# Weight splits of a float32 two-block network: six buffers instead of four for each split half, and a scheduling priority of 150 places for weight loads and splits

## The chip, the cores and the metric

One core of a Trainium2 chip runs the whole program. The metric is the device time of one execution in microseconds (us), and the kernel before is given by three runs and one profiled execution.

## The reference, cut to what matters

A sequence of 256 tokens of width 1024 goes through two layers of a first block (a pooling branch, sparse attention that keeps the 64 best keys of each query, attention to a memory, three gated merges), then through one layer of a second block (a gated delta rule run in both directions, a short convolution branch, a gated merge) and a gated MLP. Everything is float32. Nearly all of the arithmetic is a product of activations with a weight matrix:

```python
proj = h @ w_in[l]                                   # first block, 1024 x 6728 per layer
merged = (g[:, :, 0] * (y_pool @ w_branch[l, 0]) + g[:, :, 1] * (y_attn @ w_branch[l, 1])
          + g[:, :, 2] * (y_mem @ w_branch[l, 2]))
x = x + merged @ w_out[l]
...
o_dn = gated_deltanet_bidir(q, k, v, z, b_raw, a_raw, conv_w, A_log, dt_bias, norm_w)   # second block
h_res = h_res + (silu(gu[..., :D_FF]) * gu[..., D_FF:]) @ w_down[l]                     # MLP
```

## The kernel before, in words

**A product.** Every float32 product is computed as three products of a reduced-precision type: an operand is split into a high half H (its rounded copy) and a low half L (operand minus H), and the kernel sums H·H, H·L and L·H in PSUM (`mm3`, L116 to L124; `units`, L138 to L153). The activations are split once. The weights are read from HBM once and split on the way: `load` (L92 to L95) issues a DMA from SP into one of five `raw` buffers, and `weights` (L97 to L114) lets ScalarE write H (L107) and VectorE write L (L110), into one of four `wH` and one of four `wL` buffers. A part is up to four blocks of 128 rows by 256 columns, 128x1024 elements in a buffer. A unit of work is a weight block of 1024 rows by 256 columns: two parts, 48 matmuls on TensorE, two result tiles. In the second block and the MLP every third L is written by POOL (`pool_l`, L108 and L109).

**The order of the program.** Block 1 (`_block1`, L220) goes twice through projections, attention, branches and output. It begins with DMAs of `norm_g` (L258) and of x in four pieces (L261), with the first two half parts of weights between them (`K.ahead`, L263); then x is split (`xsplit`, L284), and two units are computed side by side (L333) while POOL sums the squares of x (L188 to L194). Block 2 (`_block2`, L575) begins with q, k and v and their convolutions (`qkv`, L659, VectorE at L685), and then interleaves further units (`z_unit`, `gate`, the `w_sc` units) with a generator, `delta` (L835): decays, an inverse of triangular blocks of 32 in many small VectorE steps (`inverse_blocks`, L820 to L832), a way through DRAM and back (L946 writes, `load_inverse` L988 to L1005 reads, all from SP), and then matmuls and VectorE steps per half of the heads. The generator is advanced by `K.pump` after each unit, and drained before the output product. `_mlp` (L1264) is products almost alone.

**What sets the order on an engine.** The program is traced in that order, and each instruction takes a place from it. The framework then goes through a modelled timeline and gives each engine, whenever it is free there, the ready instruction with the lowest place; an instruction that needs a buffer is ready once a buffer of its tag is free. What comes out is a fixed queue for each engine, which the chip executes in that order: an instruction that has to wait holds up all that stand behind it on its engine, SP's DMA queue included. The kernel asks for this with `schedule_with_timeline_sim=True` in `kernel` (L1417). `issue_after` (L75 to L81) adds that certain instructions are not put ahead of the last weight load or matmul traced so far.

Of the kernel before, what the change touches and what calls it, by code (L numbers as in the profile page):

```python
# [8 lines left out]
F32R = mybir.dt.float32r  # L9
# [20 lines left out]
RATE = 2.0  # L30
POOL_L = 3
NL0 = 1


def _constants():
# [16 lines left out]
class _K:  # L52
# [43 lines left out]

    def weights(self, blk, kt, n):  # L97

        nc = self.nc
        parts = {}  # L100
        k0 = 0
        while k0 < kt:
            raw = self.ahead.pop(0) if self.ahead else self.load(blk, k0, min(4, kt - k0), n)
            m = raw.shape[1]
            H = self.wp.tile([128, 4, n], F32R, tag="wH", name="wH", bufs=4)[:, :m, :]
            L = self.wp.tile([128, 4, n], F32R, tag="wL", name="wL", bufs=4)[:, :m, :]
            nc.scalar.activation(H, raw, AF.Copy)  # L107
            self.n_l += 1  # L108
            e = nc.gpsimd if self.pool_l and self.n_l % self.pool_l == 0 else nc.vector  # L109
            e.tensor_tensor(L, raw, H.bitcast(F32), op=OP.subtract)  # L110
            for i in range(m):
                parts[k0 + i] = H, L, i
            k0 += m
        return [lambda k, a=a: parts[k][a][:, parts[k][2], :] for a in range(2)]  # L114
# [59 lines left out]
    def hl(self, pool, src, shape, tag, bufs=1):  # L174
        nc = self.nc
        H = pool.tile(shape, F32R, tag=tag + "H", name=tag + "H", bufs=bufs)
        L = pool.tile(shape, F32R, tag=tag + "L", name=tag + "L", bufs=bufs)
        nc.scalar.activation(H, src, AF.Copy)
        nc.vector.tensor_tensor(L, src, H.bitcast(F32), op=OP.subtract)
        return H, L  # L180

    def scaled_hl(self, H, L, x, g):

        nc = self.nc
        nc.scalar.activation(H, x, AF.Copy, scale=g)
        nc.vector.scalar_tensor_tensor(L, x, g, H.bitcast(F32), op0=OP.mult, op1=OP.subtract)
# [388 lines left out]
def _block2(K, x):  # L575
# [19 lines left out]

    K.pool_l, K.n_l = POOL_L, NL0

# [833 lines left out]
```

## Time and profile before

| | |
|---|---|
| median of three runs | 1180.29 us (1178.58 to 1182.12) |
| the profiled execution's own time | 1179.4 us |
| its span, first to last instruction | 1177.4 us |
| mean granted TensorE clock | 0.979 |
| busy: TensorE, VectorE, ScalarE, POOL | 1114.1, 869.0, 586.7, 383.5 us |
| bytes read from HBM | 189.39 MB, 165 GB/s over the span |

The profiled execution lies 0.9 us under the median. The rows further down come from it. A busy TensorE means that matmuls are in flight; a clock of 1.00 is the higher of its two levels (2.4 GHz), and a mean below that is time at the lower one (1.2 GHz). In rows of a timeline the first two columns are the start and the duration in us, and square brackets give the idle time of the engine before the row and the instruction that ended it. In rows of waits, "A <- B: t, n, m" says that A waited for B for t us in total, n times, at most m.

### The profile page before, as it was taken

The page shows a single profiled execution, that of the slowest core. Times are in us where ns is not written, and L with a number is a line of the kernel's source. Part 1 is how long each engine was busy: PE and PEld are TensorE (multiplying, and loading weights), DVE is VectorE, ACT ScalarE, POOL GpSimd, SP SyncE. Part 2 cuts the span into 40 slices and gives each one's busy share as a digit, 9 for nine tenths or more (in the row PEclk, how much of TensorE's full clock was granted, in tenths as well). Part 3 has the DMA queues.
Part 4 walks back from the last instruction along what each step waited for, and adds up shares of the span by engine and source line. Part 5 has one row for each costly group of instructions (what it writes and reads, how often), then busy time and mean ns, then how long its engine had stood idle before and what let it go on. Part 6 is the DMA issues. An engine that isn't in the chain of part 4 may idle for free.

```text
span 1177.4 us, 23260 instructions
## 1 busy us (share of the span) xinstructions
PE 1114.1 (95%) x9536; PEld 1086.1 (92%) x9536; DVE 869.0 (74%) x1220; ACT 586.7 (50%) x883; POOL 383.5 (33%) x304
## 2 busy tenths in 40 slices
PE   6999999999999999999999878698899999999996
PEld 6999999999999999999998878697799999999996
DVE  8668897678665897977899899996547497555543
ACT  6344546446344454455675947242235645444442
POOL 8102310003100040100854668933011157534353
PEclk9999999999999999999999979898899999999999
DMA  7765453565655544455544525454432355556561
GB/s 262 268 211 170 156 173 123 180 192 182 196 192 182 179 133 136 147 177 180 186 169 144 181 82 144 134 175 105 148 126 94 134 187 180 200 172 199 180 193 40
DMA packets 68514, 194.63 MB, mean 165 GB/s; under 512 B 19504, under 2 KB 21816, under 8 KB 67896
## 3 DMA queue, kind: packets, MB, share of 16 engines
q1 hardware_dynamic: 66056, 188.72, 49.9%
q10 hardware_dynamic: 2352, 4.43, 1.1%
q8 instruction: 74, 1.21, 0.4%
q14 instruction: 32, 0.26, 0.1%
HBM read 189.39 MB, written 5.30 MB: 165 GB/s over the span
## 4 chain that ended last, share of the span: by engine, by line
PE 70%; DVE 17%; DMA 4%; issue 3%; ACT 2%; POOL 2%; SPq 1%; DVEq 0%; ACTq 0%; POOLq 0%
PE mm L123 49%; PE mml L151 8%; PE mmd L1302 5%; DVE wL L110 4%; DVE ac L685 2%; DVE Tb L830 1%; PE hp L372 1%; ACT wH L107 1%; DMA sT<-Lb 1%; DMA rows<-scr 1%; DVE tm L828 1%; DVE vf L685 1%; DVE kq L713 1%; PE mo L495 1%; PE vn L1088 1%
## 5 line engine op out<-in xcount | busy, mean ns | idle before, releaser
L110 DVE TENSOR_TENSOR wL<-raw,wH 128x1024 fp32r<-128x1024 f32 (+2 forms) x292 | 395.9, 1362 | 156.4 <-ACT wH L107 139.4
L107 ACT ACTIVATE wH<-raw 128x1024 fp32r<-128x1024 f32 (+3 forms) x347 | 347.0, 1034 | 302.4 <-PE mm L123 150.2
L123 PE MATMUL mm<-xH,wL 128*128 128x256 f32 (+3 forms) x1720 | 247.7, 284 | 11.2 <-DVE wL L110 11.2
L123 PE MATMUL mm<-xH,wH 128*128 128x256 f32 (+3 forms) x1720 | 249.0, 286 | 5.6 <-ACT ac L680 1.8
L123 PE MATMUL mm<-xL,wH 128*128 128x256 f32 (+3 forms) x1720 | 248.6, 285 | 0.0
L123 PEld LDWEIGHTS mm<-xH,wL 128*128 128x128 f32 (+1 forms) x1720 | 221.9, 190 | 13.5 <-DVE wL L110 12.3
L123 PEld LDWEIGHTS mm<-xH,wH 128*128 128x128 f32 (+1 forms) x1720 | 222.7, 190 | 9.5 <-ACT ac L680 2.0
L123 PEld LDWEIGHTS mm<-xL,wH 128*128 128x128 f32 (+1 forms) x1720 | 223.2, 191 | 2.8 <-issue 2.2
L110 POOL TENSOR_TENSOR wL<-raw,wH 128x1024 fp32r<-128x1024 f32 (+2 forms) x55 | 133.9, 2434 | 217.5 <-ACT wH L107 149.3
L397 POOL TENSOR_TENSOR bp<-bias,sc 128x1024 f32<-128x1024 f32 (+1 forms) x4 | 14.7, 3667 | 246.3 <-DVE sc L395 219.9
L123 PE MATMUL mm<-yH,wH 128*128 128x256 f32 x256 | 42.5, 286 | 4.9 <-ACT yH L1207 4.9
L123 PE MATMUL mm<-yL,wH 128*128 128x256 f32 x256 | 43.0, 286 | 4.3 <-DVE yL L1208 4.3
L123 PE MATMUL mm<-yH,wL 128*128 128x256 f32 x256 | 42.1, 285 | 0.0
L191 POOL TENSOR_TENSOR acc<-x 128x256 f32<-128x256 f32 x2 | 1.4, 722 | 123.6 <-DVE x L562 120.4
L123 PEld LDWEIGHTS mm<-yH,wH 128*128 128x128 f32 x256 | 35.6, 193 | 5.2 <-ACT yH L1207 5.1
L123 PEld LDWEIGHTS mm<-yL,wH 128*128 128x128 f32 x256 | 35.7, 193 | 5.1 <-DVE yL L1208 4.8
L123 PEld LDWEIGHTS mm<-yH,wL 128*128 128x128 f32 x256 | 35.5, 193 | 0.3 <-issue 0.3
L193 POOL TENSOR_TENSOR sq<-x 128x256 f32<-128x256 f32 x33 | 33.6, 1027 | 6.2 <-DVE x L562 5.5
L685 DVE SCALAR_TENSOR_TENSOR ac<-rc,cw,ac 128x271 f32<-128x271 f32 (+3 forms) x48 | 34.4, 753 | 0.0
L191 POOL TENSOR_TENSOR a<-x 128x256 f32<-128x256 f32 x3 | 2.8, 941 | 80.4 <-DVE x L562 74.8
L1302 PE MATMUL mmd<-aH,wH 128*128 128x256 f32 x176 | 28.6, 281 | 0.0
L1302 PE MATMUL mmd<-aH,wL 128*128 128x256 f32 x176 | 28.6, 281 | 0.0
(433 smaller groups left out, 1829.3 us busy)
## 6 DMA issues: line engine op xcount, KB each, us to landing
raw<-in_w_b SPq DMA_DIRECT2D x64, 512.0 KB, 4.1
raw<-in_w_a SPq DMA_DIRECT2D x55, 512.0 KB, 4.0
raw<-in_w_gu SPq DMA_DIRECT2D x44, 512.0 KB, 4.5
raw<-in_w_branch SPq DMA_DIRECT2D x24, 512.0 KB, 4.3
raw<-in_w_out SPq DMA_DIRECT2D x24, 512.0 KB, 3.8
raw<-in_w_qkv SPq DMA_DIRECT2D x24, 512.0 KB, 3.8
raw<-in_w_sc SPq DMA_DIRECT2D x24, 512.0 KB, 3.8
raw<-in_w_down SPq DMA_DIRECT2D x20, 512.0 KB, 4.4
```

The lines of the kernel that those rows point to most:

```text
L107: nc.scalar.activation(H, raw, AF.Copy)
L110: e.tensor_tensor(L, raw, H.bitcast(F32), op=OP.subtract)
L123: self.last_mm = nc.tensor.matmul(ps, lt(a, kt), rt(b, kt), start=i == 0, stop=i == n - 1).ins
L151: self.last_mm = self.nc.tensor.matmul(ps[:, :N], w[a](k)[:, h * 128:h * 128 + 128], xs[b][:, k, :], start=k == 0 and (a, b) == (0, 0), st ...
L193: nc.gpsimd.tensor_tensor(tmp, x, x, op=OP.mult)
L372: nc.tensor.matmul(pp[p][:, j, :n], a[r, 2 * i + j, :], b(r, 2 * i + j), start=True, stop=True)
L397: nc.gpsimd.tensor_tensor(bp[:, :, :n], bias[:, :, off:], pen[:, None, :n].to_broadcast([128, 8, n]), op=OP.add)
L495: nc.tensor.matmul(ps[:, h, :], mv[:, mb, h * 128:h * 128 + 128], PT[:, mb, h, :], start=mb == 0, stop=mb == 1)
L685: V.scalar_tensor_tensor(ac[:, t0:t1], r[:, t0 + j - 2:t1 + j - 2], w[:, j:j + 1], ac[:, t0:t1], op0=OP.mult, op1=OP.add)
L713: (V if (i * 8 + h) % 3 else G).tensor_tensor(t, t, sl(h, i), op=OP.mult)
L828: eng.tensor_tensor(t, Lb[:, j + 1:, j:j + 1].to_broadcast([P, m, w]), Tb[:, j:j + 1, 0:w].to_broadcast([P, m, w]), op=OP.mult)
L1302: nc.tensor.matmul(pss[h][:, :S], w[a](k)[:, h * 128:h * 128 + 128], (aH, aL)[b][:, k0 + k, :], start=k0 + k == 0 and (a, b) == (0, 0), st ...
```

## The change

Three edits. The body of `weights` becomes `split_weights`, and `weights` calls it with the scheduler's place of everything traced inside lowered by 150, so that a part's load (where it isn't one of the two `ahead` loads, which are issued elsewhere), its H and its L count as traced 150 instructions earlier than they were. The tags `wH` and `wL` get six buffers each instead of four; `raw` keeps five. And the region of each SBUF partition that is set aside for descriptors of DMAs issued by POOL is set to 512 bytes, which makes room for the four added buffers of 4 KB per partition each.

```diff
+AHEAD = 150
...
     def weights(self, blk, kt, n):
 
+        with self.tc.high_priority(AHEAD):
+            return self.split_weights(blk, kt, n)
+
+    def split_weights(self, blk, kt, n):
         nc = self.nc
...
-            H = self.wp.tile([128, 4, n], F32R, tag="wH", name="wH", bufs=4)[:, :m, :]
-            L = self.wp.tile([128, 4, n], F32R, tag="wL", name="wL", bufs=4)[:, :m, :]
+            H = self.wp.tile([128, 4, n], F32R, tag="wH", name="wH", bufs=6)[:, :m, :]
+            L = self.wp.tile([128, 4, n], F32R, tag="wL", name="wL", bufs=6)[:, :m, :]
...
-    nc = bacc.Bacc("TRN2", target_bir_lowering=False, num_devices=1)
+    nc = bacc.Bacc("TRN2", target_bir_lowering=False, num_devices=1, dynamic_dma_scratch_size=512)
```

## Rows read from the trace of the kernel before

**Rows 1.** The page, part 1: TensorE's busy time, share of the span and instructions.

```profile
PE 1114.1 (95%) x9536; PEld 1086.1 (92%) x9536; DVE 869.0 (74%) x1220; ACT 586.7 (50%) x883; POOL 383.5 (33%) x304
```

**Rows 2.** The table of windows, by stages: window and its length; busy us (and instructions) of TensorE, its weight loads, VectorE, ScalarE, POOL; granted clock; share of the DMA engines busy; GB/s.

```profile
0.00:60.00 60.00, 49.70 (x387) 47.26 (x387) 44.00 (x50) 30.47 (x45) 28.80 (x38) 1.00 0.78 267
60.00:480.00 420.00, 419.60 (x3566) 409.94 (x3567) 316.91 (x480) 204.07 (x311) 53.59 (x52) 1.00 0.54 171
480.00:512.00 32.00, 30.46 (x272) 29.46 (x271) 27.72 (x33) 16.50 (x33) 4.25 (x1) 1.00 0.46 147
...
585.00:805.00 220.00, 188.00 (x1409) 180.91 (x1407) 210.70 (x315) 129.58 (x223) 137.43 (x109) 0.94 0.47 148
805.00:831.00 26.00, 19.00 (x124) 17.28 (x125) 11.60 (x20) 7.19 (x11) 4.52 (x4) 0.80 0.58 156
831.00:990.00 159.00, 156.26 (x1677) 151.68 (x1677) 105.49 (x152) 72.75 (x96) 50.91 (x29) 0.98 0.41 134
```

**Rows 3.** Waits of TensorE in the stretch 585 to 831 us, the five longest in total.

```profile
PE mm L123 <- DVE wL L110: 8.6, 3, 5.6
PE ms L984 <- ACT mkv L980: 5.5, 1, 5.5
PE mm L123 <- ACT yH L1207: 4.9, 1, 4.9
PE mvn L979 <- DVE mkv L976: 4.7, 1, 4.7
PE mm L123 <- DVE yL L1208: 4.3, 1, 4.3
```

**Rows 4.** Waits over the whole span: what ScalarE's H split waited for most.

```profile
ACT wH L107 <- PE mm L123: 150.2, 68, 5.2
```

**Rows 5.** The chain of waits over the whole span (start, us, what): a stretch of TensorE in the MLP without a wait, in which 960 matmuls are 20 units.

```profile
991.52 113.06 PE mm L123 x960
```

**Rows 6.** Timeline of VectorE, 685 to 742 us: a convolution step that was held up, and the L split behind it.

```profile
694.61 7.43 DVE L685 SCALAR_TENSOR_TENSOR vf<-rc,cw,vf 128x270 f32<-128x270 f32 x1
701.96 1.29 DVE L110 TENSOR_TENSOR wL<-raw,wH 128x1024 fp32r<-128x1024 f32 x1
```

**Rows 7.** Timeline of POOL around the same moment: the first and the last but one of the six operations that it ran without a gap from 694.76 to 702.17 us.

```profile
694.76 1.89 POOL L897 TENSOR_TENSOR E<-Gb,Gt 128x1024 f32<-128x1024 f32 x1
...
699.41 2.33 POOL L110 TENSOR_TENSOR wL<-raw,wH 128x1024 fp32r<-128x1024 f32 x1
```

**Rows 8.** Timeline of TensorE: the product that waited for that L split.

```profile
703.30 1.23 PE L123 MATMUL mm<-xH,wL 128*128 128x258 f32 x4 [5.57 <-DVE wL L110]
```

**Rows 9.** SP's DMA issues around 805 us (start, us): the inverse on its way to DRAM and back (L946, L998 to L1003), and the next weights.

```profile
804.26 1.18 SPq L946 DMA_DIRECT2D sT<-Tb  x2
...
819.27 0.48 SPq L1000 DMA_DIRECT2D TBX<-sT  x1
...
823.22 0.98 SPq L94 DMA_DIRECT2D raw<-in_w_gate  x2
```

**Rows 10.** The chain of waits, 800 to 835 us (start, us, what).

```profile
805.49 11.27 DMA sT<-Lb
...
823.22 4.75 DMA raw<-in_w_gate
...
829.04 0.58 ACT mkv L980
```

**Rows 11.** Waits of ScalarE, 800 to 832 us.

```profile
ACT wH L107 <- DMA raw<-in_w_gate: 8.0, 1, 8.0
```

**Rows 12.** Waits of TensorE, 50 to 580 us.

```profile
PE mm L123 <- ACT wH L107: 0.8, 1, 0.8
PE mm L123 <- DVE wL L110: 0.7, 1, 0.7
```

**Rows 13.** SP's DMA issues at the start (start, us): the first piece of x, and the three whole parts of the two first units.

```profile
1.19 0.41 SPq L261 DMA_DIRECT2D x<-in_xT  x1
...
4.01 1.81 SPq L94 DMA_DIRECT2D raw<-in_w_a  x3
```

**Rows 14.** ScalarE at the start: the split of the first piece of x, and those of the first and the last of the three whole parts of weights, each begun when its data landed (the second began at 11.88 us).

```profile
4.48 0.91 ACT L185 ACTIVATE xH<-x,ng 128x256 fp32r<-128x256 f32 x2 [2.25 <-DMA x<-in_xT]
...
10.41 1.06 ACT L107 ACTIVATE wH<-raw 128x1024 fp32r<-128x1024 f32 x1 [0.33 <-DMA raw<-in_w_a]
...
13.24 1.39 ACT L107 ACTIVATE wH<-raw 128x1024 fp32r<-128x1024 f32 x2 [0.30 <-DMA raw<-in_w_a]
```

**Rows 15.** TensorE at the start: the first product, and the sum over the squares of x, which stands behind the last of the 96 products of the two first units.

```profile
6.30 0.79 PE L151 MATMUL mml<-xH,wH 128*128 128x256 f32 x2 [6.30 <-ACT wH L107]
...
21.09 0.59 PE L201 MATMUL stat<-acc,ones 128*128 128x256 f32 x2
```

**Rows 16.** Waits of TensorE, 0 to 60 us.

```profile
PE mm L123 <- DVE wL L110: 1.9, 2, 1.3
```

**Rows 17.** The L split (L110) on VectorE: count, ns min/median/max, first and last start.

```profile
L110 DVE TENSOR_TENSOR wL<-raw,wH x292: 351/1222/4916, 6.3 to 1154.7; 128x1024 fp32r<-128x1024 f32 x142, 128x288 fp32r<-128x288 f32 x2, 128x512 fp32r<-128x512 f32 x1, 128x192 fp32r<-128x192 f32 x1
```

**Rows 18.** The DMA queues (packets, MB, share of 16 engines): the two that carry what the program issues, from SP and from ScalarE; the list of issues by line names no other engine.

```profile
q1 hardware_dynamic: 66056, 188.72, 49.9%
q10 hardware_dynamic: 2352, 4.43, 1.1%
```

## The prediction

> **What bounds the kernel now.** I began with the page [rows 1]: TensorE is busy 1114.1 of 1177.4 us, so 63.3 us idle are all that better feeding can win, with the clock that idling costs. The table by stages [rows 2] says where they lie. From 60 to 480 us TensorE is busy 419.6 of 420: there buffers and places are worth nothing. From 0 to 60 us it lacks 10.3, from 480 to 512 us 1.5, from 585 to 805 us 32.0 and from 805 to 831 us 7.0. In the long one VectorE is busy 210.7 of 220 us: VectorE bounds it. In the one after it VectorE is busy 11.6 of 26: there a way through DRAM bounds it. Granted clocks of 0.94 and 0.80 cost another 13.2 and 5.2 us of full speed (0.06 x 220, 0.20 x 26). From 831 us TensorE is nearly full again (156.3 of 159).
>
> Next, who ended the waits of TensorE from 585 to 831 us [rows 3]. Only 8.6 us of the 39.0 are waits for an L split. Another 5.5 are for `mkv`, which turns out below to stand behind a weight load. The y splits (9.2) and the other `mkv` (4.7) are VectorE's and ScalarE's own work, and no buffer brings them sooner.
>
> Do four buffers bind? Yes: the H split waited 150.2 us in 68 waits for TensorE to give a buffer back [rows 4]. A unit takes two parts of the four, so the splits are one unit ahead of TensorE, and two with six. A unit lasts 5.65 us (113.06 / 20) [rows 5]: that is the added cover.
>
> **The change part by part.**
>
> *Six buffers in the VectorE-bound stretch.* The longest wait shows the mechanism. A convolution step held VectorE for 7.43 us, and the L split behind it began at 701.96 us [rows 6], while POOL ran six operations without a gap [rows 7]; the product waited 5.57 us for it [rows 8]. One unit more of finished splits covers it, just (5.65 against 5.57), and the two shorter waits of the 8.6 too. But the same held VectorE also empties PSUM, so a TensorE that has its weights may next wait for a result tile. Ends: 0 (all 8.6 become waits for tiles) and 8.6. I take 5.0, nearer the upper end, since each result tile has half a unit of matmuls before it is needed again.
>
> *A weight load behind the inverse.* SP sent the inverse out from 804.26 us, read it back until 823.12, and issued the next weights only at 823.22 [rows 9]. They landed 4.75 us later, and the `mkv` copy ran at 829.04 behind their split [rows 10]: ScalarE had waited 8.0 us for that load [rows 11], and TensorE 5.5 for the copy. With two more parts split, two `raw` buffers come free earlier and their loads can be issued before SP turns to the inverse. Late next is the inverse itself: its reads were issued until 823.12 us and the first product that needs them follows `mkv`. Ends: 0 and 5.5. I take 4.0: nearer the upper end, since the spare unit of 5.65 us covers it, and short of it, since that unit may be used up by then.
>
> *480 to 512 us.* Two waits for splits, 1.5 us together [rows 12], with TensorE full after them. Ends 0 and 1.5; I take 1.0.
>
> *The place of 150 at the start.* Here the change costs. SP now issues x first (1.19 us) and the three whole parts of the first two units from 4.01 us [rows 13]. These parts are traced within some 40 instructions of the start, so minus 150 puts them ahead of all x pieces, which keep their places, as the two `ahead` halves do. The data of these three parts landed 1.42 us apart ((13.24 - 10.41) / 2) [rows 14]; three of them push x back by 4.2 us, and the first product from 6.30 to 10.5 us. But the two first units took from 6.30 to 21.09 us [rows 15] for 96 matmuls that are worth 11.3 (two units), since they waited for their data: 3.5 us of slack. Left are 0.7 us. Waits for splits from 20 to 31 us, 1.9 us [rows 16], may go as well. Ends: 1.2 gained, 4.2 lost. I enter 0.7 lost.
>
> *The place of 150 further on.* For loads it decides little: SP issues a load as soon as a `raw` buffer is free, and there are still five. For L splits it means that they pass convolutions, evictions and the inverse's steps on VectorE. In a stretch that VectorE bounds this is paid once, not per unit, as buffers fill only once: two parts more before the inverse is done, 2 x 1.22 us [rows 17], and every reader of the inverse later by that. Two loads more ahead of the inverse on SP add the 0.98 us that two take to issue [rows 9]. On POOL and ScalarE the same moves are hidden, as both are busy under two thirds of the stretch. Ends: 0 (the extra parts are split before 585 us, where VectorE has room) and 3.4. I take 1.5.
>
> A row and a rule differ on one price here. The row says that VectorE was held for 7.43 us by a run of POOL's operations, of which the longest shown took 2.33 [rows 6, 7]. So a POOL split that is pulled into such a run would lengthen the hold by its own 2.33 us; I count that in the upper end of the range only. The Trainium skill, page "SBUF — State Buffer", section "Who interferes with whom", says that the shared ports are locked for one whole instruction and that the one issued first holds them: by that rule a hold ends with one POOL operation, and a longer run would add nothing. The trace disagrees with its 7.43 us.
>
> *The descriptor region.* All DMAs are on the queues of SP and ScalarE [rows 18]; none issued by POOL could want the region. Cost 0.
>
> Sum: 5.0 + 4.0 + 1.0 - 0.7 - 1.5 = 7.8 us less than the profiled 1179.4, so 1171.6. The median of the runs lies 0.9 higher; carried over, the forecast is 1172.5 us. I leave the clock out of the sum: TensorE would still idle some 30 us in the stretch.
>
> **The rivals.**
>
> *Slower: x comes late.* The three loads ahead of x cost their full 4.2 us, as the sums of squares on POOL also start at x and everything later in block 1 needs them, and TensorE is full from 60 us, so nothing is regained until 480. It decides if the gains in 585 to 831 us stay under it. For it: the kernel begins at SP, and no gain there is certain. Against it: the 3.5 us of slack. With none of the gains: 1180.3 + 4.2 = 1184.5; with the 3.4 of the inverse, 1187.9.
>
> *No difference: VectorE bounds it anyway.* The change removes no VectorE work, and 210.7 of 220 us are taken. The waits for L become waits for result tiles, and the inverse ends when it did. For it: 30 of the 39 us of idling wait for other work already. Result: the start's 0.7 lost, and one of the small gains, 1180 +- 3.
>
> *More than forecast.* All covered waits go (8.6 + 5.5 + 1.5 + 1.2 = 16.8), no cost is paid, and TensorE, with fewer gaps, gets back part of the 18.4 us at the low clock: 1163.5 without clock, some 1154 with half of it. For it: gaps and low clock lie in the same stretch. Against it: VectorE's share.
>
> *The change doesn't do what it says*: the scheduler may find the buffers unused, since its own clock decides when a split is ready. The row of 150.2 us speaks against that; its time is the one of no difference, and its chance is in there.
>
> **How the numbers follow.** Forecast 0.42 (1163 to 1176), more than forecast 0.13, no difference 0.20, slower 0.25, the last high because every queue is rearranged and a wait that lands on an engine in order holds all behind it. About 0.3% (3.5 us) is what a measurement of this kernel can tell from no change, so faster 0.55, same 0.20, slower 0.25. The range takes the forecast, the lower half of the gain beyond it and most of the slower case: 1157 to 1187.
>
> **What would show it.** The table by stages of the changed kernel: 60 to 480 us as full as before; the stretch of the second block (585 to 831) shorter by about 9 us; TensorE's waits for L near 0 there, and no `mkv` behind a weight load. SP's first issues: three whole parts, then x; first product at about 10.5 us. I am wrong if waits for L stay (then buffers weren't the limit), if waits for result tiles or `yL` grow by as much (VectorE), if the sum at 60 us is later by over 2 us (the start), or if the inverse leaves later than by 3.4 us.

## The result, and the profile after

The change made the kernel slower: 1189.5 us (median of five runs; 1187.1 to 1191.7) against 1181.7 (1178.6 to 1182.5) for the kernel before beside it, a ratio of 1.0075 with a 95% interval of 1.0055 to 1.0095. I had forecast 1172.5 and a range of 1157 to 1187. The profiled execution took 1187.1 us (span 1185.3). Single executions far outside the rest, of 1544 us (kernel before), 2778 us (e4) and 3150 us (e9), are in none of the ratios below.

The table of windows, the stages of [rows 2]:

```profile
0.00:60.00 60.00, 48.88 (x359) 46.65 (x360) 41.88 (x49) 29.52 (x44) 27.17 (x38) 0.94 0.77 263
60.00:480.00 420.00, 419.38 (x3565) 409.71 (x3564) 317.34 (x475) 205.86 (x314) 53.39 (x51) 1.00 0.53 172
480.00:512.00 32.00, 31.19 (x272) 30.62 (x270) 29.67 (x41) 17.72 (x34) 4.71 (x1) 1.00 0.44 142
...
585.00:805.00 220.00, 188.80 (x1409) 182.00 (x1407) 206.93 (x301) 127.54 (x222) 142.28 (x108) 0.95 0.46 145
805.00:831.00 26.00, 22.82 (x168) 21.23 (x168) 21.38 (x40) 11.05 (x16) 10.79 (x6) 0.87 0.52 157
831.00:990.00 159.00, 146.99 (x1574) 142.62 (x1575) 93.62 (x146) 66.70 (x90) 39.93 (x24) 0.96 0.41 132
```

From 585 to 831 us TensorE idles 34.4 us instead of 39.0: less, as forecast. What loses is the stage that I had called nearly full and left out of the sum: from 831 to 990 us TensorE issues 1574 products instead of 1677.

Waits of TensorE from 585 to 831 us, against [rows 3]:

```profile
PE mm L129 <- DVE cS L1194: 10.7, 3, 5.5
PE mm L129 <- DVE rc L678: 7.9, 2, 5.2
PE mm L129 <- DVE cv L1212: 5.5, 1, 5.5
...
PE mvn L985 <- DVE mkv L982: 1.6, 1, 1.6
```

No wait for an L split is left among them, and none for an `mkv` behind a weight load. In their place stand 24.1 us of waits for VectorE's evictions and convolutions (`cS`, `rc`, `cv`), of which 1.7, for `cv`, were there before.

To see where the time goes I add up TensorE's work from the trace: each product counts its columns (64 at least) at 2.4 GHz plus 9 ns, about what full stretches show (355 or 342 products of 256 columns in 40 us). The difference of the sums at the same moment is a kernel's **lag** behind the kernel before, in us of TensorE work. Change of the lag by stage:

| us | forecast | the change |
|---|---|---|
| 0 to 100 | +0.7 | +3.8 |
| 100 to 580 | -1.0 | -1.6 |
| 580 to 900 | -7.5 | 0.0 |
| 900 to 1000 | none | +5.6 |
| sum | -7.8 | +7.8 |

Inside 580 to 900 the lag rises by 5.7 up to 620, falls by 11.3 up to 830, and rises by 5.5 again up to 900. The gain that I had forecast did come; it was paid for before and after. From 830 us on, where I had forecast nothing, 11.1 us are lost in all. One profile is not the median: a run with the order of the kernel before (e11, below) shows up to 1.5 us in a stage of this table that its median doesn't, and inside the third stage 2.6 us down to 830 us and up again.

**The last stage.** TensorE at the end of the delta rule (`ks`, `vn`, `o`), and what follows it:

```profile
923.11 1.11 PE L129 MATMUL mm<-xH,wL 128*128 128x256 f32 x8
924.05 0.39 PE L1094 MATMUL vn<-vb,TT 128*128 128x128 f32 x2
...
926.45 0.49 PE L1094 MATMUL vn<-vb,TT 128*128 128x128 f32 x2 [0.44 <-DVE vb L1090]
...
930.52 0.71 PE L1129 MATMUL o<-At,vb 128*128 128x128 f32 x4 [0.69 <-ACT vb L1095]
...
945.08 1.19 PE L157 MATMUL mml<-oHL,wH 128*128 128x256 f32 x8 [1.57 <-ACT wH L113]
...
965.38 5.19 PE L157 MATMUL mml<-mHL,wH 128*128 128x256 f32 x29 [2.55 <-ACT mHL L191]
```

The same end in the kernel before:

```profile
923.59 0.61 PE L1123 MATMUL o<-At,vb 128*128 128x128 f32 x4
923.95 0.48 PE L123 MATMUL mm<-xH,wL 128*128 128x256 f32 x2
924.27 1.10 PE L123 MATMUL mm<-xH,wH 128*128 128x256 f32 x8
...
929.75 1.10 PE L123 MATMUL mm<-xL,wH 128*128 128x256 f32 x8
930.69 1.10 PE L123 MATMUL mm<-xH,wL 128*128 128x256 f32 x8
931.63 1.09 PE L151 MATMUL mml<-oHL,wH 128*128 128x256 f32 x8
```

Before, unit products (`mm`) lie between and behind the last steps and fill the time in which VectorE and ScalarE norm and split the result. After, the last unit product stands at 923.11 us, ahead of them, and each step's wait is bare. Behind the wait of 2.55 us the granted clock was low as well (0.83 on average from 960 to 970 us): the next 29 products took 5.19 us, against 3.4 at the 117 ns of a full stretch, so part of them ran at 1.2 GHz.

Why they ended earlier is in the order of instructions, which is fixed when the kernel is built: the scheduler takes, by its own clock, what is ready. Counted there, 82 products of units stand behind the last `ks` in the kernel before, 58 behind the last `vn` and 50 behind the last `o`; in the changed kernel none; the traces show the same counts. Two more buffers made the units ready earlier.

**The stage before it.** VectorE at the start of block 2, after and before:

```profile
587.25 5.69 DVE L116 TENSOR_TENSOR wL<-raw,wH 128x1024 fp32r<-128x1024 f32 x3
592.87 1.84 DVE L641 RECIPROCAL St<-sd 128x272 f32<-128x272 f32 x1
```

```profile
583.35 1.49 DVE L110 TENSOR_TENSOR wL<-raw,wH 128x192 fp32r<-128x192 f32 x2
585.20 1.85 DVE L635 RECIPROCAL St<-sd 128x272 f32<-128x272 f32 x1 [0.36 <-ACT sd L89]
```

Three whole L splits pass the scale `St`, from which convolutions and the delta rule start. SP's issues of the inverse, against [rows 9]:

```profile
813.70 1.18 SPq L952 DMA_DIRECT2D sT<-Tb  x2
...
825.79 0.44 SPq L96 DMA_DIRECT2D raw<-in_w_gate  x1
```

It leaves at 813.70 us, 9.4 later than before, and a weight load is issued among its reads. TensorE has two waits of over 1 us in the products behind it:

```profile
832.48 0.31 PE L1022 MATMUL x<-Tn,LT 32*32 32x32 f32 x2 [1.32 <-DMA Tn<-sT]
...
844.74 0.25 PE L1030 MATMUL t<-TBX,TT 32*32 32x32 f32 x1 [4.82 <-issue]
```

Only the first is for the inverse on its way back. The second, 4.82 us and so most of the 5.5 lost from 830 to 900 us, has no releaser in the profile; the last section comes back to it.

**The start.** SP's issues, against [rows 13], and the first product, against [rows 15]:

```profile
2.12 0.43 SPq L267 DMA_DIRECT2D x<-in_xT  x1
2.59 1.99 SPq L96 DMA_DIRECT2D raw<-in_w_a  x4
4.62 0.99 SPq L267 DMA_DIRECT2D x<-in_xT  x2
```

```profile
6.33 0.79 PE L157 MATMUL mml<-xH,wH 128*128 128x256 f32 x2 [6.33 <-ACT wH L113]
```

Weights passed only the third and fourth piece of x, and the first product is not late. Still the lag is 2.9 us at 40 us. The window from 30 to 40 us, after and before:

```profile
30.00:40.00 10.00, 9.64 (x54) 9.04 (x55) 10.00 (x14) 4.53 (x6) 4.60 (x5) 0.66 0.71 224
```

```profile
30.00:40.00 10.00, 9.53 (x75) 8.35 (x76) 8.56 (x13) 2.71 (x5) 3.92 (x4) 1.00 0.72 246
```

TensorE is as busy in both, but after the change at a granted clock of 0.66, with 21 products fewer (2.5 us at 117 ns). Ahead of it lie short waits, 3.3 us together from 24 to 31 us; the kernel before has 2.8 us of them and kept 1.00.

### The profile page after: what moved, and what is told of

Its sections match the earlier page's. It is cut to its first block, busy times and chain, and to the rows that moved or that the text cites. A ratio compares the mean times of both kernels' runs of the same rounds, so it can differ in the third digit from the quotient of the medians.

```text
span 1185.3 us, 23294 instructions
## 1 busy us (share of the span) xinstructions
PE 1117.4 (94%) x9536; PEld 1090.9 (92%) x9536; DVE 863.0 (73%) x1220; ACT 584.6 (49%) x883; POOL 386.2 (33%) x304
## 4 chain that ended last, share of the span: by engine, by line
PE 74%; DVE 15%; issue 3%; DMA 3%; ACT 2%; SPq 1%; POOL 1%; DVEq 0%; ACTq 0%; POOLq 0%
PE mm L129 50%; PE mml L157 10%; PE mmd L1308 5%; DVE wL L116 3%; DVE ac L691 2%; DVE Tb L836 2%; DVE tm L834 1%; PE hp L378 1%; DMA rows<-scr 1%; DMA x<-in_xT 1%; PE kkq L912 1%; PE mo L501 1%; PE vn L1094 1%; PE o L1125 1%; ACT wH L113 1%
## 5 line engine op out<-in xcount | busy, mean ns | idle before, releaser
L116 DVE TENSOR_TENSOR wL<-raw,wH 128x1024 fp32r<-128x1024 f32 (+2 forms) x292 | 402.5, 1385 | 155.1 <-ACT wH L113 152.5
L129 PE MATMUL mm<-xH,wH 128*128 128x256 f32 (+3 forms) x1720 | 252.4, 288 | 26.3 <-DVE cS L1194 10.7
L691 DVE SCALAR_TENSOR_TENSOR ac<-rc,cw,ac 128x271 f32<-128x271 f32 (+3 forms) x48 | 30.5, 670 | 0.0
```

The source lines that it names most:

```text
L129: self.last_mm = nc.tensor.matmul(ps, lt(a, kt), rt(b, kt), start=i == 0, stop=i == n - 1).ins
L691: V.scalar_tensor_tensor(ac[:, t0:t1], r[:, t0 + j - 2:t1 + j - 2], w[:, j:j + 1], ac[:, t0:t1], op0=OP.mult, op1=OP.add)
```

## The experiments

Theories. **A (order)**: the number of buffers changes the fixed order, and units that end earlier leave the delta rule's end uncovered. **B (place)**: the place of 150 puts splits ahead of the delta rule's steps. **C (late chain)**: the delta rule is late, and that alone counts. Ratios are to the kernel before on the same chip, with 95% intervals; "behind" counts unit products behind the last `ks`. `RATE` (2.0 in both kernels) sets how much of the delta rule is traced after each unit: a higher one puts its steps ahead of more units. Three names come up besides: `Smem`, a scale for the memory's tokens; `rows` and `bias`, two transfers by which ScalarE spreads a table in DRAM and fetches it; `mHL`, the split halves of the merged branches.

**e1**, six buffers and the region, without the priority:

```
-        with self.tc.high_priority(AHEAD):
-            return self.split_weights(blk, kt, n)
+        return self.split_weights(blk, kt, n)
```

> Six buffers and the region of 512 stay, the priority of 150 goes. Theory A (order): it is the number of buffers that changes the fixed order of work on each engine; in the new order no unit product stands on TensorE behind the delta rule's last ks products (82 did before), so nothing covers the end of the delta rule. Then the start is as before (TensorE's lag at 60 us back from 3.3 us to under 0.5), the loss from 920 to 990 us stays near 8, and the time is 4 to 7 us over the kernel before (the change: 7.8 over). Theory B (place): the place of 150 put splits ahead of the delta rule's VectorE steps; then without it the inverse leaves near 804 us again, the tail is covered, and the time is 3 to 8 us under the kernel before, as I forecast for the buffers.

1187.1 us, 1.0060 (1.0044 to 1.0076). B falls: without the priority nearly all of the loss stays, and so does the order on TensorE from the 107th instruction on. From 900 to 1000 us the lag grows by 6.0. The start was not as expected: level at 60 us, then 6.8 lost by 80.

**e2**, the change with four buffers (`bufs=6` back to `bufs=4`, twice):

> The change with four buffers instead of six; priority and region stay. Theory A (order): the place of 150 moves only the first loads, so TensorE lags by about 3 us from 40 us to 480 us, and what follows is as before: 1.5 to 3.5 us over the kernel before, all of it the start. Theory B (place): the splits still pass the delta rule's VectorE work, so the inverse leaves several us later and the time is 6 to 9 us over. If the region cost anything, it would be seen here as time in every stage, not only up to 60 us.

1184.3 us, 1.0036 (1.0023 to 1.0049). As A has it: from 580 to 900 us nothing is lost (-1.6), and at the end 1.9, with 83 behind. The loss is larger than I expected, by under 1 us, and spread up to 300 us.

**e3**, six buffers without the priority, `RATE = 2.5`:

> Six buffers without the priority, and RATE raised from 2.0 to 2.5: more of the delta rule is written down per unit, so 56 unit products stand behind its last ks products again (0 in the change, 82 before) while VectorE's order around the start of block 2 stays that of the change (189 splits ahead of the scale St, 186 before). Theory A (order): the loss from 920 to 990 us goes by 56 of 82, some 6 of 8 us; 0 to 4 us under the kernel before. Rival C (the chain is late because three splits of 5.69 us stand ahead of St, and its end sets the time whatever TensorE does meanwhile): no better than six buffers alone, 4 to 7 us over.

1181.6 us, 1.0000 (0.9979 to 1.0022). Against e1 it wins 0.6%; the lag grows by 2.0 from 900 to 1000 us instead of 6.0, although VectorE has as many splits ahead of `St` (189). C falls.

**e4**, five buffers without the priority:

> Five buffers without the priority: 31 unit products stand behind the last ks products (82 with four, 0 with six), 7 behind the last vn products (58 and 0), none behind the last o (50 and 0). Theory A (order): the loss at the end of the delta rule lies between those of four and six, nearer six: 2 to 6 us over the kernel before. Rival C (splits ahead of St): in proportion to VectorE's delay at the start of block 2, half of that of six, 2 to 4 over. Theory B (place): 2 to 6 us under, as five buffers give part of the gain and there is no priority.

1182.8 us, 1.0009 (0.9992 to 1.0025). Its end loses 4.7, as A has it, but the whole is better than the 2 to 6 us expected. In its profile little is lost at the start (0.9 up to 100 us); whether that is the fifth buffer's doing is not shown, as this loss varies between runs of one order (1.7 in e3, 6.8 in e1).

**e5**, the whole change with `RATE = 2.5`:

> The whole change (six buffers, region, priority of 150) with RATE 2.5 instead of 2.0: 56 unit products stand behind the delta rule's last ks products, 32 behind the last vn, 24 behind the last o (0, 0, 0 in the change). Theory A (order; no unit product is left to cover the end of the delta rule): the loss from 920 to 990 us falls from 8 us to 2 or 3, what is left is the start, and the time is 2 to 5 us over the kernel before. Rival C (the chain is late, and that alone counts): still 6 to 8 us over.

1183.3 us, 1.0030 (1.0010 to 1.0049): as A has it.

**e6**, six buffers, `RATE = 2.5`, and splits held back at the start of block 2:

```
+    K.hold = K.conv              # last convolution step of qkv(1, 1)
     qkv(1, 2)
+    K.hold = None
...
+                with self.tc.issue_after(self.hold):
+                    e.tensor_tensor(L, raw, H.bitcast(F32), op=OP.subtract)
```

> Six buffers without the priority, RATE 2.5, and the two L splits of the unit qkv(1, 2) are kept behind the first convolutions on VectorE (issued after them), so that 185 splits stand ahead of the scale St (189 in the change, 186 before) and 102, 78 and 70 unit products behind the last ks, vn and o. Theory A: the delta rule's end is covered better than in the kernel before (82, 58, 50), its steps are no longer late by 9 us, and the waits for L from 660 to 720 us are still gone: 2 to 8 us under the kernel before. Rival D (TensorE starves from 585 to 620 us while the held splits wait, and what the buffers gain later is lost there): within 3 us of the kernel before.

1197.9 us, 1.0145 (1.0121 to 1.0169). Rival D, and worse than it said: 12 us are lost from 580 to 640 us, while TensorE waits 8.3 us for a held split and 8.3 us for evictions (`rc`), and hardly any of it comes back. At the end 4.7 are lost in spite of 102 products behind, in one wait of 4.75 us for `mHL`: cover for the delta rule's end does not help the branch behind it.

**e7**, the kernel before with the last four gate units raised:

```
+        with K.tc.high_priority(400):
+            gate(0, g_)
-        gate(0, g_)
```

> The kernel before, four buffers and no priority of weights; only the last four gate units are raised by 400 places, so that their products stand ahead of the delta rule's last steps: 0 unit products behind the last ks, vn and o (82, 58, 50 before). Up to there TensorE's order is that of the kernel before (the first 6671 of 8929 instructions). Theory A (order): this alone costs what the change lost at its end, 5 to 9 us over the kernel before, all of it after 900 us. Rival C (the change lost because the delta rule was late; what stands behind its end does not matter): within 2 us of the kernel before.

1186.9 us, 1.0046 (1.0028 to 1.0065). This is theory A by itself: four buffers, no priority of weights, the lag within 1.7 us of level up to 900 us, -0.1 there, and 5.0 at 1000. The window 905 to 990 us, first of the kernel before, then of this one, then of the change:

```profile
905.00:990.00 85.00, 82.57 (x695) 80.10 (x694) 59.42 (x81) 44.84 (x62) 37.58 (x24) 1.00 0.50 162
```

```profile
905.00:990.00 85.00, 79.15 (x661) 76.26 (x660) 60.99 (x82) 41.51 (x59) 32.51 (x22) 1.00 0.45 149
```

```profile
905.00:990.00 85.00, 79.13 (x652) 76.84 (x652) 56.52 (x85) 40.70 (x58) 30.14 (x20) 0.98 0.44 146
```

34 products fewer with the order alone, 43 with the change.

**e8**, the kernel before with `RATE = 2.5`:

> The kernel before with RATE 2.5 alone: 125, 101 and 93 unit products behind the last ks, vn and o (82, 58, 50 before). It tells what of a gain of six buffers with RATE 2.5 is RATE's own. Theory A: the end of the delta rule was covered already but for short waits (1.1 us and less), so 0 to 3 us under the kernel before. If cover was still short there, 4 us under or more.

1185.9 us, 1.0040 (1.0025 to 1.0055): slower, against my expectation. 125 products stand behind, and give nothing at an end that was covered; 5.3 us are lost from 580 to 900 us. I put that down to the delta rule's steps, which now stand ahead of units on a full VectorE; that is argued, not shown. So RATE is no gain by itself; it pays with six buffers only.

**e9**, e3 with the `bias` transfer issued later by ScalarE:

```
-        nc.scalar.dma_start(out=bias, ...)          # in build_bias
+            with tc.issue_after(K.last_act):        # behind the copy smt
+                load_bias()
```

> Six buffers, RATE 2.5, no priority, and ScalarE issues the bias transfer later: behind the copy smt, not between the weight splits, so that ScalarE does not stand still from 49 to 59 us until the rows transfer has landed. Theory S (the six-buffer kernels lose their first 2 to 7 us at this wait: the splits behind it are late, and TensorE waits for Smem 4.6 to 5.4 us or has had a low clock before): TensorE's lag at 100 us falls under 1 us (2.8 with the same order otherwise, 6.8 and 7.4 in two other six-buffer profiles), and the time is 1 to 4 us under that of the same kernel with the early issue (1181.6), so 0 to 4 under the kernel before. Rival (the wait is covered by split weights, and the low clock after a short gap is what costs): lag at 100 us still 1.7 or more, time unchanged.

1178.0 us, **0.9975 (0.9963 to 0.9987)**: faster than both kernels by a little, the only one here. ScalarE in e1, where the start lost 6.8 us, and TensorE's wait behind it:

```profile
47.10 2.01 ACT L112 ACTIVATE wH<-raw 128x1024 fp32r<-128x1024 f32 x2 [4.78 <-PE mm L128]
58.03 0.41 ACTq L255 DMA_DIRECT2D bias<-rows  x1
58.89 2.00 ACT L112 ACTIVATE wH<-raw 128x1024 fp32r<-128x1024 f32 x2 [9.79 <-PE mm L128]
```

```profile
PE tok L217 <- DVE Smem L209: 5.4, 1, 5.4
```

The label of 9.79 us names TensorE, but what ended it was the issue at 58.03, which had waited for the `rows` transfer; the splits stand behind it in order, and `Smem` behind them. In e9:

```profile
50.95 2.01 ACT L112 ACTIVATE wH<-raw 128x1024 fp32r<-128x1024 f32 x2 [3.06 <-issue]
52.86 0.46 ACT L208 ACTIVATE sd<-stat,eps 128x256 f32<-128x256 f32 x1
...
59.43 0.40 ACTq L256 DMA_DIRECT2D bias<-rows  x1
```

The splits run 8 us earlier, TensorE has no wait for `Smem`, and the lag at 100 us is -1.5.

**e10**, e4 with `RATE = 2.5`:

> Five buffers, RATE 2.5, no priority: 54, 30 and 22 unit products behind the last ks, vn and o (31, 7, 0 with five and RATE 2.0). Theory A (order): five buffers alone lost 5.4 us of TensorE work between 920 and 980 us; with the cover back it loses 2 or so, and the time is 1 to 5 us under five alone (1182.8), from 4 under to 1 over the kernel before. Rival C: as five buffers alone.

1183.9 us, 1.0035 (1.0010 to 1.0060): a miss. It lost 5.5 at the end with 54 behind. Its runs spread from 1176.2 to 1193.8, and the profiled one is the slowest of them; why they spread is open, part of the 5.5 is the clock (below).

**e11**, the kernel before with the region alone:

> The kernel before with the descriptor region of 512 bytes alone; every engine's order is that of the kernel before. All theories: no difference, within 2 us of the kernel before. A loss of 3 to 4 us here would take the place of the first loads as the reason for the 4 us that the change with four buffers lost.

1180.8 us, 1.0001 (0.9989 to 1.0013). The region costs nothing; it is what makes room for the buffers. (The Trainium skill, page "SBUF — State Buffer", section "SBUF size: 192, 224, or 256?", has 16 KiB of each partition set aside for descriptors; four more parts of 4 KiB come to as much, and no run here shows the size.)

**e12**, e3 with `POOL_L = 2`:

> Six buffers, RATE 2.5, no priority, and every second L split of block 2 on POOL instead of every third: 14 splits of 1.22 us leave VectorE (17 us), and POOL takes them at 2.60 us each. Theory V (VectorE bounds block 2 from 585 to 831 us, and with six buffers it is the evictions and the delta rule, not the splits, that TensorE waits for): the stretch gets shorter by 3 to 8 us, and the time is 2 to 7 us under the same kernel with every third (1181.6). Rival P (POOL's longer splits come late or hold VectorE, as in the row of 7.43 us): no gain, or slower by up to 6.

1201.2 us, 1.0170 (1.0146 to 1.0195): rival P, and beyond its 6 us, as it is 20 us over e3. From 580 to 900 us 12.8 are lost. VectorE's share is not bought off with POOL's splits.

**e13** and **e14**, the change with the late `bias` transfer, at RATE 2.0 and at 2.5; **e15**, the kernel before with it:

> The whole change, and only the bias transfer issued behind the copy smt on ScalarE. Theory S (part of the change's loss is ScalarE standing still for this transfer while the next splits queue behind it): 2 to 4 us under the change, so 4 to 6 over the kernel before; the end of the delta rule is uncovered as before and still loses its 5 to 7 us from 920 to 990 us. Rival (the loss at the start is three weight parts ahead of x, as I forecast): no difference to the change, 7 to 8 over.

> The whole change with RATE 2.5 and the late bias transfer. If the change's 7.8 us are the uncovered end of the delta rule (6.2 came back with RATE 2.5 alone) and the wait on ScalarE, nothing is left: 2 under to 1 over the kernel before. Against the same kernel without the priority (1178.0) it gives the price of the place of 150, first loads ahead of x included: 0.7 by my forecast of that term, 3 to 4 by the kernel with four buffers and the priority.

> The kernel before with the late bias transfer alone. Theory S: in the kernel before ScalarE stands still there too, but with four buffers no split could have been made ahead in that time, as it was waiting for TensorE to give a buffer back, and TensorE waited only 0.8 us for Smem: 0 to 1.5 us under the kernel before. If it gains 3 or more, the gain of the six-buffer kernel with the late transfer is not the buffers' at all.

e13: 1184.7 us, 1.0027 (1.0012 to 1.0043), some 5 us under the change; its end still loses 5.4. e14: 1181.7, 1.0007 (0.9993 to 1.0021), some 3 us under e5. e15: 1180.7, 1.0000 (0.9990 to 1.0009): with four buffers the wait is free.

Put together (per cent over the kernel before; 0.1 is 1.2 us):

| | RATE 2.0 | RATE 2.5 | RATE 2.5, late bias |
|---|---|---|---|
| four buffers | 0 | +0.40 | not run |
| six buffers | +0.60 | 0.00 | -0.25 |
| six and the priority | +0.75 | +0.30 | +0.07 |

Not in the table: at RATE 2.0 with the late transfer four buffers have 0.00 and six with the priority +0.27; four buffers with the priority have +0.36; five buffers +0.09, and +0.35 at RATE 2.5.

Growth of the lag from 900 to 1000 us by the products behind: none (the change, e1, e7, e13) 5.6, 6.0, 5.1, 5.4; 31 (e4) 4.7; 56 (e3, e5, e9, e14) 2.0, 3.6, 2.0, 2.9; 83 (e2) 1.9; 125 (e8) 1.3. Out of line are e10 (5.5 with 54), e6 (4.7 with 102) and e12 (4.3 with 149). The clock accounts for these: from 900 to 1000 us the granted clock is 0.97 in the three, 1.00 in e3, e7 and e9, and 0.98 in the other runs of this list. With 0.03 and 0.02 of the 100 us taken off, the growth is 3.4 to 5.1 with none behind, 2.7 with 31, 2.5 with 54, 0.9 to 2.0 with 56, and -0.7 to 1.7 with 83 and more. The low clock comes behind waits, so it is in part a cost of the same thing; but the three are no counterexamples.

## Why the prediction was wrong

**The step that failed** is "From 831 us TensorE is nearly full again". I took a stage that was full as one that could not lose, and put it at nothing in the sum; in the profile 11.1 us are lost from 830 to 1000 us. Half of that is shown. The stage was full at the end of the delta rule because the fixed order had kept 82 unit products for it; buffers that let units end earlier take that cover away. It cost 5.6 us in the profile after 900 us, 5 to 7 us by the runs (e5 against the change, e3 against e1; RATE may move a little elsewhere too), and e7 shows it without any of the change. The other half, 5.5 us from 830 to 900 us, is for the most part the wait of 4.82 us without a releaser, and its cause stays open. No rival of mine had it: all moved work within the order that I had read.

**Six buffers in the VectorE-bound stretch (-5.0), and the load behind the inverse (-4.0).** Both waits went, and from 620 to 830 us the lag fell by 11.3. It was given back on both sides: 5.7 at the start of block 2, and 5.5 in the products behind the inverse, which left 9.4 us later, against the 3.4 by which I would call myself wrong. From 580 to 900 us the net is 0.0 (-1.2 in e1, -1.8 in e3, -1.6 in e9). That looks like my rival "VectorE bounds it anyway", and the sign that I had named for it, waits for result tiles that grow by as much, is in the list of waits above: half a unit of matmuls before a tile is needed again, my reason for 5.0, was not enough. But the wait of 4.82 us is not VectorE's by any row. That two splits more would be paid once, 2 x 1.22 us, missed that three of them stand ahead of the one operation from which the whole delta rule starts, and took 1.90 us each there.

**480 to 512 us (-1.0).** Right: 1.5 from 480 to 580 us, and 1.3 to 1.6 in every profile with five or six buffers. With four buffers it is at most 0.2, but for 2.1 in e7, which ran there at the faster of two paces (last section).

**The place of 150 at the start (+0.7).** The picture was wrong: two pieces of x, not four, were passed, and the first product came at 6.33 us, not 10.5. The size was inside my ends, by luck: 0.15, 0.30 and 0.32% (e1, e3 and e9 against the same with the priority; the first is inside the two intervals), 2 to 4 us. Where it arises is not settled; the profile of the change is 3.2 us late at 60 us, over the 2 us that I had set as a sign, and e2 loses its 0.36% spread up to 300 us.

**The place of 150 further on (+1.5).** It was the buffers that let splits pass the delta rule, not the place: e1 has the same splits ahead of `St`.

**Not in the sum: ScalarE's wait for the `rows` transfer.** 3 to 6 us by the runs (e9 against e3, e14 against e5, e13 against the change). With four buffers the late transfer lets the next split begin 3.6 us sooner (50.94 us in e15, 54.54 before), but TensorE had waited only 0.8 us for `Smem`. With six buffers it waited up to 5.4 us (e1). In the change's own profile it waited 0.5 us; that run had lost 2.9 us by 40 us, at the low clock of the window above. e3 shows that too (0.70 from 30 to 40 us, 2.4 us lost by 40), and e1, of the same order there, kept 1.00 and lost its 6.8 at `Smem`. So a run loses at the one place or the other; what decides it stays open.

**The region (0).** Right.

## What to carry to other kernels

More buffers change not only when a transfer can start but, where a scheduler writes the order, which work is left at the end: before adding them, ask what fills the engine beside the last serial chain, and count it in the order after the change. A stage that is full may be full of borrowed work. When run-ahead grows, an instruction that waits in an in-order queue (here a transfer issued by ScalarE) starts to cost, though it cost nothing before.

## What the runs showed of the hardware that I had not expected

TensorE has two paces at a granted clock of 1.00. The MLP in the kernel before, and in e3:

```profile
1060.00:1100.00 40.00, 40.00 (x342) 40.00 (x341) 20.45 (x21) 17.94 (x22) 18.94 (x9) 1.00 0.61 197
```

```profile
1060.00:1100.00 40.00, 40.00 (x355) 40.00 (x354) 22.72 (x21) 20.01 (x25) 19.34 (x9) 1.00 0.55 178
```

117.0 ns a product against 112.7, with the same instructions and no wait. A pace lasts for tens to hundreds of us; in e3 it was worth 5.8 us of lag from 1000 to 1150 us, which is most of why its profiled execution (1173.5 us) lies 8 us under its median. (The Trainium skill, page "TensorE: Matmul & The Clock Gate", section "Back-to-back issue gap", has a formula for a product by itself, which comes to an estimate of 109 ns for 256 columns, and says that pairs of a weight load and a product are spaced otherwise; both paces here lie above that estimate.) What sets the pace stays open. So does the wait without a releaser in the products of the inverse. Ten of the eleven profiles with five or six buffers have one of 2.6 to 4.8 us, between 834 and 850 us; those with four buffers have none. In each of the ten a transfer of 16 KB on the queue that the profile calls "instruction" begins during the wait and ends 1.3 to 1.6 us before it does (in the change it begins at 842.3 us, for the product at 844.74). That points at TensorE waiting for its next instructions; no run tests it.
